# A hybrid SSD and attention layer: two products of each SSD chunk placed behind the copy of B on VectorE

## The chip, the cores and the metric

The kernel runs on one core of a Trainium2 chip. The metric is device time in microseconds (us), given as the median of several executions. The engines are called by the profile's names: PE (TensorE), DVE (VectorE), ACT (ScalarE), POOL (GpSimd) and SP (SyncE, which only issues DMAs here). PEld is PE's weight load.

## The reference, cut to what matters

One layer for 1024 tokens of width 1024: a Mamba-2 mixer (SSD) and multi-head latent attention side by side, merged by gates, then a gated MLP. The change lies in the SSD. For each of 4 groups (8 heads of 64 channels, a state of 128) the sequence is taken in 8 chunks of 128 tokens:

```python
seg = a_cum[..., :, None] - a_cum[..., None, :]
decay_in = jnp.exp(jnp.where(causal, seg, -jnp.inf))
scores = jnp.einsum('bclgn,bcsgn->bcgls', cc, bc)
y_diag = jnp.einsum('bcgls,bcgels,bcsgep->bclgep', scores, decay_in, xc)
chunk_states = jnp.einsum('bclgn,bcgel,bclgep->bcgepn', bc, decay_to_end, xc)
y_off = jnp.einsum('bclgn,cbgepn,bcgel->bclgep', cc, prev, jnp.exp(a_cum))
```

## The kernel before, in words

All products are in float32, most of them as three passes with operands split into a high and a low part (`mm3`, lines 175 to 177). So PE has long runs of 128x512 matmuls, named `lin` after their PSUM tile. The weights of a `lin` tile come by DMA into `wraw` (issued by SP, line 160), ACT casts them to the high part `whi` (line 153), and POOL subtracts to get the low part `wlo` (line 154).

In the SSD stage the loop runs over 4 groups and in each over 8 chunks; I write (g, c) for group g and chunk c. `ssd_steps` calls three functions in turn. `ssd_inputs` for the next chunk lets PE transpose x into `xp` and B into `sp` and form the scores; then DVE makes `xdt` (line 855), the masked scores `sm` (847), `xde` (860), the copy `bt` of B (863) and the product `seg` of decays and scores (864). ACT takes the exponential of `abc` (866), and DVE multiplies it by C (867). `ssd_state` is the PE product `sn` of `bt` and `xde` (874) that adds to the state (DVE, 881). `ssd_output` is the run of PE products `yp` (891 and 896) from `seg` and `abc`, then line 903 on DVE. Between these calls PE is given `lin` matmuls of other work: the convolution inputs of the next group (`conv_tile`, with lines 808 to 817 on ACT and DVE), z tiles (330) and, in the last group, tiles of the attention output (`mla_tiles`, with casts on line 146, subtractions on line 148 and line 1034).

`ssd_finish` runs a Newton iteration for the norm of the group before or of this group's first half: nine small DVE steps on 128x4 elements (lines 123 to 125, three times), called small steps below.

The order on an engine is not the order of the program text. A scheduler places each instruction by its own estimate of when inputs are ready, and every engine then works strictly in that order. `behind(name)` adds a dependence without a semaphore: the instruction just written must come later in its engine's order than the one named. PE's order is fixed in this way over the whole program (lines 1563 to 1570).

Of the kernel before, what the change touches and what calls it, by code (L numbers as in the profile page):

```python
# [72 lines left out]
def tile_hybrid_layer(ctx: ExitStack, tc: tile.TileContext, x, cols, cons, w_main, w_small, w_uq, w_ukv,  # L73
# [53 lines left out]
    def behind(name):  # L127

        ins = nc.cur_bb.bb.instructions[-1]
        if name:  # L130
            tc.add_manual_dep(ins, name, mybir.DependencyInfo(
                mybir.DependencyClass.NoSync, mybir.DependencyReason.DATA), reason="order")
        return ins.name

    def last(engine):
        return [ins for ins in nc.cur_bb.bb.instructions if ins.engine == engine][-1].name
# [635 lines left out]
    with tc.tile_pool(name="dp", bufs=2) as dp, tc.tile_pool(name="psx", bufs=1, space=PSUM) as psx, \  # L772
# [10 lines left out]
        def abc_load(n):  # L783

            if n < GROUPS * NT:
                g, c = divmod(n, NT)
                t = dp.tile([P, 8, P], F32, name="abc", bufs=3)
                nc.gpsimd.dma_start(out=t, in_=ac_d[c, 8 * g:8 * g + 8, :].partition_broadcast(P))
                abcs.append(t)
# [42 lines left out]
        def ssd_inputs(g, c):  # L832
            Bt, Ct, xs = chan[16 + g], chan[20 + g], chan[g]
            cs = slice(c * P, (c + 1) * P)
            hs = slice(8 * g, 8 * g + 8)
            abc_load(g * NT + c + 1)
            abc = abcs.pop(0)
            xp = psx.tile([P, 512], F32, name="xp")
            for j in range(4):
                PE.transpose(xp[:, j * P:(j + 1) * P], xs[:, j, cs], ident)  # L840
            sp = psx.tile([P, 512], F32, name="sp")
            PE.matmul(sp[:, 0:P], lhsT=Bt[:, cs], rhs=Ct[:, cs], start=True, stop=True)
            if c < NT - 1:
                PE.transpose(sp[:, 256:384], Bt[:, cs], ident)

            sm = dp.tile([P, P], F32, name="sm_")
            V.scalar_tensor_tensor(sm, sp[:, 0:P], 0.25, tri, op0=ALU.mult, op1=ALU.mult)
            seg = dp.tile([P, 8, P], F32, name="seg")
            for hd in range(8):
                S.activation(seg[:, hd, :], abc[:, hd, :], AF.Relu, bias=acum[:, c, 8 * g + hd:8 * g + hd + 1],  # L850
                             scale=-1.0)
            S.activation(seg, seg, AF.Exp, scale=-1.0)
            xv = xp.rearrange("p (h d) -> p h d", d=64)
            xdt = dp.tile([P, 512], F32, name="xdt")
            V.tensor_tensor(xdt.rearrange("p (h d) -> p h d", d=64), xv,
                            dtt[:, c, hs].unsqueeze(2).broadcast_to([P, 8, 64]), op=ALU.mult)
            xde = bt = None
            if c < NT - 1:
                xde = dp.tile([P, 512], F32, name="xde")
                V.tensor_tensor(xde.rearrange("p (h d) -> p h d", d=64), xv,  # L860
                                dte[:, c, hs].unsqueeze(2).broadcast_to([P, 8, 64]), op=ALU.mult)
                bt = dp.tile([P, P], F32, name="bt")
                V.tensor_copy(bt, sp[:, 256:384])
            V.tensor_tensor(seg, seg, sm.unsqueeze(1).broadcast_to([P, 8, P]), op=ALU.mult)
            if c > 0:
                S.activation(abc, abc, AF.Exp)
                V.tensor_tensor(abc, abc, Ct[:, cs].unsqueeze(1).broadcast_to([P, 8, P]), op=ALU.mult)
            return abc, seg, xdt, xde, bt

        def ssd_state(g, c, inp, st):  # L870
# [48 lines left out]
        def ssd_steps(g):  # L919
            st = None  # L920
            nxt = ssd_inputs(g, 0)
            yield
            for c in range(NT):
                inp = nxt
                nst = None
                if c < NT - 1:
                    nst = ssd_state(g, c, inp, st)
                    if c:
                        ssd_squares(g, c - 1)
                    yield  # L930
                    nxt = ssd_inputs(g, c + 1)
                    yield
                else:
                    ssd_squares(g, c - 1)
                ssd_output(g, c, inp, st)
                st = nst
                yield
# [129 lines left out]
        for n, _ in enumerate(conv_group(0)):  # L1067
# [3 lines left out]
            if n == 33:  # L1071
                name = last(mybir.EngineType.DVE)
# [581 lines left out]
```

## Time and profile before

| | |
|---|---|
| Median of 3 runs | 2227.03 us (2224.92 to 2229.38) |
| The profiled execution, its own time | 2224.44 us |
| Its span | 2222.6 us |
| PE busy | 2173.7 us, 98% of the span |
| DVE busy | 1430.4 us, 64% |
| ACT, POOL busy | 1012.4 us (46%), 822.4 us (37%) |
| Mean granted clock of PE | 0.996 of full speed |

The profiled execution took 1.8 us more than its span. Times in the rows count from the start of the span; the SSD stage lies between 800 and 1260 us.

### The profile page before, as it was taken

To read this page: it belongs to the slowest core of one execution; us is meant where nothing else is said; L and a number is where in the kernel's file an instruction comes from. 1 tells how busy PE (TensorE), PEld (TensorE's weight loads), DVE (VectorE), ACT (ScalarE), POOL (GpSimd) and SP (SyncE) were. 2 spreads that over 40 slices of the span, in tenths; PEclk is the share of its full clock that TensorE was granted. 3 is DMA by queue.
4 is the path that set the end of the run, shared out by engine and by line. 5 is a ranking of instruction groups with operands and counts; after the bars stand their busy time and mean duration, and the time that the engine had idled before them with its cause. 6 is when DMAs were issued, how large, how long until landed. Compare 5 with 4: busy or idle time off the path is not lost.

```text
span 2222.6 us, 31323 instructions
## 1 busy us (share of the span) xinstructions
PE 2173.7 (98%) x11488; PEld 1765.2 (79%) x11488; DVE 1430.4 (64%) x2496; ACT 1012.4 (46%) x1852; POOL 822.4 (37%) x911
## 2 busy tenths in 40 slices
PE   8999999999999999999999999999899999999999
PEld 6777777777777887878878889889688888888887
DVE  4466656666672469898876746546977777764432
ACT  5345454445444346666554424335544444443320
POOL 2244423443343237665455311012555555510000
PEclk9999999999999999999999999999999999999999
DMA  4121111111213224544276566543222222247531
GB/s 146 54 68 49 40 48 63 50 45 39 69 43 130 68 76 152 181 162 167 95 227 207 178 223 203 166 162 95 67 95 86 81 81 86 76 142 246 201 130 67
DMA packets 112714, 253.57 MB, mean 114 GB/s; under 512 B 13168, under 2 KB 19248, under 8 KB 112560
## 3 DMA queue, kind: packets, MB, share of 16 engines
q1 hardware_dynamic: 99008, 210.54, 28.6%
q0 software_dynamic: 11008, 37.76, 5.3%
q10 hardware_dynamic: 2544, 3.28, 0.4%
q8 instruction: 90, 1.47, 0.3%
q14 instruction: 64, 0.52, 0.1%
HBM read 194.63 MB, written 56.89 MB: 113 GB/s over the span
## 4 chain that ended last, share of the span: by engine, by line
PE 75%; DVE 13%; ACT 4%; DMA 3%; issue 2%; POOL 1%; SPq 0%; DVEq 0%; ACTq 0%; POOLq 0%
PE lin L175 12%; PE lin L177 12%; PE lin L176 12%; PE dps L177 8%; PE dps L175 8%; PE dps L176 8%; PE pv L670 2%; PE s L175 2%; PE s L176 1%; PE s L177 1%; PE s L627 1%; PE yp L891 1%; PE sn L874 1%; DMA wraw<-in_w_ssd 1%; DVE qk L588 1%
## 5 line engine op out<-in xcount | busy, mean ns | idle before, releaser
L175 PE MATMUL lin<-h,whi 128*128 128x512 f32 x1440 | 592.4, 411 | 0.0
L177 PE MATMUL lin<-h,wlo 128*128 128x512 f32 x1440 | 564.0, 392 | 0.0
L176 PE MATMUL lin<-h,whi 128*128 128x512 f32 x1440 | 563.0, 391 | 0.0
L175 PEld LDWEIGHTS lin<-h,whi 128*128 128x128 f32 x1440 | 271.4, 188 | 81.6 <-issue 33.4
L177 PEld LDWEIGHTS lin<-h,wlo 128*128 128x128 f32 x1440 | 270.7, 188 | 59.8 <-DVE wlo L154 0.2
L176 PEld LDWEIGHTS lin<-h,whi 128*128 128x128 f32 x1440 | 271.9, 189 | 53.2 <-issue 7.0
L153 ACT CAST whi<-wraw 128x512 fp32r<-128x512 f32 x276 | 166.6, 619 | 281.4 <-PE lin L176 131.6
L154 POOL TENSOR_TENSOR wlo<-wraw,whi 128x512 fp32r<-128x512 f32 x134 | 192.1, 1450 | 185.1 <-ACT whi L153 177.6
L659 ACT ACTIVATE e<-s 128x512 f32<-128x512 f32 (+1 forms) x192 | 93.7, 493 | 164.6 <-DVE s L657 137.7
L664 POOL TENSOR_TENSOR acc<-acc,e 128x512 f32<-128x512 f32 (+3 forms) x80 | 79.6, 995 | 230.8 <-ACT e L659 217.7
L154 DVE TENSOR_TENSOR wlo<-wraw,whi 128x512 fp32r<-128x512 f32 x142 | 99.2, 714 | 94.4 <-ACT whi L153 94.3
L154 DVE TENSOR_TENSOR h<-ar,h 128x1024 fp32r<-128x1024 f32 x40 | 48.7, 1225 | 108.8 <-ACT h L153 108.7
L850 ACT ACTIVATE seg<-abc,acum 128x128 f32<-128x128 f32 x256 | 80.6, 392 | 48.3 <-PE yp L891 42.3
L153 ACT CAST h<-ar 128x1024 fp32r<-128x1024 f32 x40 | 42.1, 1056 | 124.8 <-PE lin L176 115.7
L176 PE MATMUL dps<-wlo,h 128*128 128x512 f32 x240 | 93.4, 389 | 0.0
L175 PE MATMUL dps<-whi,h 128*128 128x512 f32 x240 | 93.4, 389 | 0.0
L177 PE MATMUL dps<-whi,h 128*128 128x512 f32 x240 | 93.4, 389 | 0.0
L812 DVE SCALAR_TENSOR_TENSOR xg<-craw,cl,xg 128x1024 f32<-128x1024 f32 x48 | 73.8, 1537 | 27.4 <-ACT xg L810 26.9
L664 DVE TENSOR_TENSOR acc<-acc,e 128x512 f32<-128x512 f32 (+3 forms) x80 | 53.5, 668 | 41.0 <-ACT e L659 40.4
L1140 ACT CAST xhi<-ur 128x512 fp32r<-128x512 f32 (+1 forms) x41 | 34.1, 832 | 89.5 <-PE dps L176 79.5
L670 PE MATMUL pv<-e,vt 128*64 128x512 f32 (+3 forms) x384 | 72.9, 499 | 0.0
L175 PE MATMUL s<-qh,kh 97*128 97x512 f32 (+1 forms) x192 | 68.5, 357 | 2.0 <-ACT qh L644 1.1
(587 smaller groups left out, 5189.5 us busy)
## 6 DMA issues: line engine op xcount, KB each, us to landing
wraw<-in_w_main SPq DMA_DIRECT2D x112, 256.0 KB, 3.1
ur<-in_w_up SPq DMA_DIRECT2D x44, 512.0 KB, 3.5
ar<-a_d SPq DMA_DIRECT2D x40, 512.0 KB, 5.1
abc<-ac_d POOLq DMA_DIRECT2D x32, 512.0 KB, 5.2
wraw<-in_w_ssd SPq DMA_DIRECT2D x64, 256.0 KB, 2.8
wraw<-in_w_down SPq DMA_DIRECT2D x44, 256.0 KB, 3.8
a_d<-uc SPq DMA_DIRECT2D x22, 512.0 KB, 2.6
g_d<-lt SPq DMA_DIRECT2D x32, 256.0 KB, 2.8
```

Source lines behind the costliest of these rows:

```text
L153: S.copy(hi, raw)
L154: (eng or V).tensor_sub(lo, raw, hi.bitcast(F32))
L175: PE.matmul(ps, lhsT=ah, rhs=bh, start=first, stop=False, **more)
L176: PE.matmul(ps, lhsT=ah, rhs=bl, start=False, stop=False, **more)
L177: PE.matmul(ps, lhsT=al, rhs=bh, start=False, stop=last, **more)
L588: V.tensor_tensor(qk[:, :, 2 + hd, 0:64], qk[:, :, 2 + hd, 0:64], rr[:, :, 2 + hd:3 + hd].broadcast_to([P, 4, 64]), op=ALU.mult)
L659: S.activation(e[:, c0:512], ps[:, 0:w], AF.Exp)
L664: (V if hd else G).tensor_tensor(accs[hd][:, c0:512], accs[hd][:, c0:512], e[:, c0:512], op=ALU.add)
L670: PE.matmul(pv[hd * 64:(hd + 1) * 64, c0:512], lhsT=vt[:, j, hd * 64:(hd + 1) * 64], rhs=es[hd][:, c0:512], start=first, stop=last)
L812: V.scalar_tensor_tensor(c, raw[:, k:k + T], col(cw + k), c, op0=ALU.mult, op1=ALU.add)
L850: S.activation(seg[:, hd, :], abc[:, hd, :], AF.Relu, bias=acum[:, c, 8 * g + hd:8 * g + hd + 1], scale=-1.0)
L1140: S.copy(hi, r)
```

## The change

The instruction written last before the product of line 864 is the copy `bt` (in chunk 7, which has none, the product `xdt`). Both are on DVE. The two DVE products, `seg` and `abc`, must now come behind it in DVE's order. No arithmetic changes, and PE's order is the same.

```diff
                 bt = dp.tile([P, P], F32, name="bt")
                 V.tensor_copy(bt, sp[:, 256:384])
+
+            name = behind(None)
             V.tensor_tensor(seg, seg, sm.unsqueeze(1).broadcast_to([P, 8, P]), op=ALU.mult)
+            behind(name)
             if c > 0:
                 S.activation(abc, abc, AF.Exp)
                 V.tensor_tensor(abc, abc, Ct[:, cs].unsqueeze(1).broadcast_to([P, 8, P]), op=ALU.mult)
+                behind(name)
             return abc, seg, xdt, xde, bt
```

Below the change the line numbers rise: 864 becomes 866, 866 becomes 869, 867 becomes 870, and later ones rise by 4.

DVE at (0,6), before. The small steps of the first half's norm stand among the steps of the chunk:

```order
L867 TENSOR_TENSOR abc<-abc,chan 128x1024
L124 TENSOR_TENSOR rsa<-rsa,grr 128x4
L125 SCALAR_TENSOR_TENSOR grr<-rsa,grr 128x4
L855 TENSOR_TENSOR xdt<-xp,dtt 128x512
L123 SCALAR_TENSOR_TENSOR rsa<-grr,rsv 128x4
L847 SCALAR_TENSOR_TENSOR sm__8880<-sp,cn 128x128
L124 TENSOR_TENSOR rsa<-rsa,grr 128x4
L860 TENSOR_TENSOR xde<-xp,dte 128x512
L125 SCALAR_TENSOR_TENSOR grr<-rsa,grr 128x4
L863 COPY bt<-sp 128x128
```

And DVE at the same place with the change:

```order
L125 SCALAR_TENSOR_TENSOR grr<-rsa,grr 128x4
L123 SCALAR_TENSOR_TENSOR rsa<-grr,rsv 128x4
L124 TENSOR_TENSOR rsa<-rsa,grr 128x4
L125 SCALAR_TENSOR_TENSOR grr<-rsa,grr 128x4
L855 TENSOR_TENSOR xdt<-xp,dtt 128x512
L847 SCALAR_TENSOR_TENSOR sm__8880<-sp,cn 128x128
L860 TENSOR_TENSOR xde<-xp,dte 128x512
L863 COPY bt<-sp 128x128
L866 TENSOR_TENSOR seg<-seg,sm__8880 128x1024
L870 TENSOR_TENSOR abc<-abc,chan 128x1024
```

The `abc` product moved from ahead of `xdt` to behind `seg`, and all nine small steps now stand ahead of `xdt`, where three stood before. At (1,6) six stand ahead of it now, and three did before.

DVE at (3,0), the first chunk of the last group, before:

```order
L330 SCALAR_TENSOR_TENSOR lt<-lt,lin 128x512
L867 TENSOR_TENSOR abc<-abc,chan 128x1024
L148 TENSOR_TENSOR h<-lt,h 128x512
L1034 SCALAR_TENSOR_TENSOR rb<-rb,lin 128x512
L855 TENSOR_TENSOR xdt<-xp,dtt 128x512
L847 SCALAR_TENSOR_TENSOR sm__11491<-sp,cn 128x128
L860 TENSOR_TENSOR xde<-xp,dte 128x512
L863 COPY bt<-sp 128x128
```

And with the change:

```order
L330 SCALAR_TENSOR_TENSOR lt<-lt,lin 128x512
L148 TENSOR_TENSOR h<-lt,h 128x512
L1038 SCALAR_TENSOR_TENSOR rb<-rb,lin 128x512
L855 TENSOR_TENSOR xdt<-xp,dtt 128x512
L847 SCALAR_TENSOR_TENSOR sm__11491<-sp,cn 128x128
L860 TENSOR_TENSOR xde<-xp,dte 128x512
L863 COPY bt<-sp 128x128
```

The `abc` product that stood here belongs to the next chunk, (3,1), and now follows that chunk's `seg`.

ACT somewhat ahead of (3,0), before, from the last exponential of `seg` in group 2:

```order
L852 ACTIVATE seg<-seg 128x1024
L914 ACTIVATE sq__11378<-xg 128x512
L329 ACTIVATE lt<-lin 128x512
L146 CAST h<-rb 128x512 x3
L153 CAST whi<-wraw 128x512 x2
L850 ACTIVATE seg<-abc,acum 128x128 x5
```

And with the change:

```order
L852 ACTIVATE seg<-seg 128x1024
L153 CAST whi<-wraw 128x512
L329 ACTIVATE lt<-lin 128x512
L146 CAST h<-rb 128x512
L918 ACTIVATE sq__11378<-xg 128x512
L146 CAST h<-rb 128x512 x2
L153 CAST whi<-wraw 128x512
L850 ACTIVATE seg<-abc,acum 128x128 x8
```

The first of the two weight casts moved from behind three casts of `h` to directly behind the exponential. On POOL the first of the two subtractions (line 154) and on SP the first of the two weight loads that follow (line 160) moved ahead in the same way.

## Rows read from the trace of the kernel before

**Rows 1.** The page: busy time, share of the span, instructions.

```profile
PE 2173.7 (98%) x11488; PEld 1765.2 (79%) x11488; DVE 1430.4 (64%) x2496; ACT 1012.4 (46%) x1852; POOL 822.4 (37%) x911
```

**Rows 2.** Waits, 800 to 1260 us: waiter, releaser, us in total, times, longest.

```profile
PE sn L874 <- DVE bt L863: 5.1, 3, 3.1
...
PEld sn L874 <- DVE bt L863: 6.8, 4, 3.5
```

**Rows 3.** Timeline of PE: start, duration, line, operation, [idle before, releaser].

```profile
884.95 1.13 PE L874 MATMUL sn<-xde,bt 128*128 128x512 f32 x2
...
954.72 1.12 PE L874 MATMUL sn<-xde,bt 128*128 128x512 f32 x2 [0.47 <-DVE bt L863]
...
996.18 1.13 PE L874 MATMUL sn<-xde,bt 128*128 128x512 f32 x2 [1.58 <-DVE bt L863]
...
998.54 0.39 PE L175 MATMUL lin<-h,whi 128*128 128x512 f32 x1
...
1152.95 1.75 PE L874 MATMUL sn<-xde,bt 128*128 128x512 f32 x2 [3.07 <-DVE bt L863]
...
1156.92 0.39 PE L175 MATMUL lin<-h,whi 128*128 128x512 f32 x1
```

**Rows 4.** Windows: length, busy of PE, PEld, DVE, ACT, POOL, granted clock.

```profile
996.00:1000.00 4.00, 3.82 (x15) 2.83 (x16) 3.97 (x8) 0.04 (x1) 0.00 (x0) 1.00 0.67 197
1153.00:1157.00 4.00, 4.00 (x9) 2.56 (x10) 4.00 (x4) 1.62 (x3) 3.39 (x4) 0.57 0.68 196
```

**Rows 5.** Groups of DVE, 795 to 1260 us: busy, mean ns, idle before.

```profile
L867 DVE TENSOR_TENSOR abc<-abc,chan 128x1024 f32<-128x1024 f32 x27 | 35.0, 1297 | 12.6 <-ACT abc L866 12.6
...
L860 DVE TENSOR_TENSOR xde<-xp,dte 128x512 f32<-128x512 f32 x28 | 19.0, 680 | 0.0
```

**Rows 6.** Timeline of DVE at (3,0).

```profile
1148.64 1.47 DVE L867 TENSOR_TENSOR abc<-abc,chan 128x1024 f32<-128x1024 f32 x1 [3.18 <-ACT abc L866]
1150.03 0.68 DVE L148 TENSOR_TENSOR h<-lt,h 128x512 fp32r<-128x512 f32 x1
...
1151.23 0.68 DVE L855 TENSOR_TENSOR xdt<-xp,dtt 128x512 f32<-128x512 f32 x1
...
1152.62 0.28 DVE L863 COPY bt<-sp 128x128 f32<-128x128 f32 x1
```

**Rows 7.** Timeline of ACT ahead of (3,0).

```profile
1137.57 0.62 ACT L153 CAST whi<-wraw 128x512 fp32r<-128x512 f32 x1
...
1147.02 0.62 ACT L153 CAST whi<-wraw 128x512 fp32r<-128x512 f32 x1 [2.29 <-DMA wraw<-in_w_mla]
...
1148.51 0.60 ACT L146 CAST h<-lt 128x512 fp32r<-128x512 f32 x1
```

**Rows 8.** Timeline of POOL and of SP's queue ahead of (3,0).

```profile
1140.09 1.30 POOL L154 TENSOR_TENSOR wlo<-wraw,whi 128x512 fp32r<-128x512 f32 x1
...
1141.42 0.33 SPq L160 DMA_DIRECT2D wraw<-in_w_mla  x1
```

**Rows 9.** Timeline of DVE at (1,6).

```profile
990.35 1.21 DVE L867 TENSOR_TENSOR abc<-abc,chan 128x1024 f32<-128x1024 f32 x1
991.48 1.25 DVE L124 TENSOR_TENSOR rsa<-rsa,grr 128x4 f32<-128x4 f32 x1
...
993.90 0.68 DVE L855 TENSOR_TENSOR xdt<-xp,dtt 128x512 f32<-128x512 f32 x1
...
995.11 0.15 DVE L124 TENSOR_TENSOR rsa<-rsa,grr 128x4 f32<-128x4 f32 x1
...
995.84 0.28 DVE L863 COPY bt<-sp 128x128 f32<-128x128 f32 x1
```

**Rows 10.** Timeline of POOL at (1,6): the first of two `wlo`, then both merged.

```profile
990.37 2.34 POOL L154 TENSOR_TENSOR wlo<-wraw,whi 128x512 fp32r<-128x512 f32 x1
...
990.37 3.59 POOL L154 TENSOR_TENSOR wlo<-wraw,whi 128x512 fp32r<-128x512 f32 x2
```

**Rows 11.** Timeline of DVE at (0,6) and at (1,3).

```profile
884.62 0.28 DVE L863 COPY bt<-sp 128x128 f32<-128x128 f32 x1
...
947.95 2.28 DVE L812 SCALAR_TENSOR_TENSOR chan<-craw,cl,chan 128x1024 f32<-128x1024 f32 x1 [0.77 <-ACT chan L810]
```

## The prediction

> **What bounds the kernel now.** I read the page's busy times first: PE is busy for 2173.7 us of a span of 2222.6 us [rows 1]. Its `lin` matmuls follow each other without a break, so a change on DVE can only win or lose time where PE stops, or where its clock drops. PE's order is the same in both kernels. So the next view is what PE waited for in the SSD stage. There is one entry: the state product `sn` waited for the copy `bt`, 5.1 us in 3 places; counted at its weight loads it is 6.8 us in 4 places [rows 2]. Between these two figures lies all that PE loses to DVE in this stage. The timeline of PE gives the places: 0.47 us at (1,3), 1.58 us at (1,6), 3.07 us at (3,0), and at (0,6) a start 0.05 us after `bt` ended at 884.90 us, with almost no idle time of PE [rows 3, 11]. The other 24 `sn` had their `bt` in time.
>
> The longest stop costs more than itself. After it the granted clock is 0.57 over 4 us, about the lower of PE's levels (1.2 GHz, and 2.4 GHz at 1.00); after the stop of 1.58 us it stayed at 1.00 [rows 4]. From the start of `sn` to the third `lin` product of line 175 behind it took 1156.92 - 1152.95 = 3.97 us there, and 998.54 - 996.18 = 2.36 us at (1,6) [rows 3]. The slow clock cost about 1.6 us.
>
> **What the change does.** The tie of `seg` does nothing by itself: it stood behind `bt` already. What moves is the `abc` product, from ahead of the chunk's `xdt` to behind its `seg`. It takes 1.30 us on average in 27 of its 28 places, and DVE also stood still ahead of it for 12.6 us in total, until ACT's exponential was done [rows 5]. That idle time held up everything behind it on DVE, `bt` above all. At the new place the product comes some 3 us later (`xdt`, `sm`, `xde`, `bt` and `seg` run first), and the longest wait was 3.18 us [rows 6], so I cost the wait at the new place at nothing. If ACT were late all the same, what would queue behind the product is line 903 (which frees the PSUM of `yp`) and the convolution steps of line 812, for which ACT's line 816 and then its copies of `lin` wait. The consumer of `abc` itself, the second products of `yp`, come after the next `sn`, many microseconds later, except in chunk 7, where `abc` will end about when `seg` did before.
>
> Four places, one after the other.
>
> (3,0). Before, DVE waits 3.18 us for ACT and then spends 1.47 us on a product of the next chunk, ahead of the steps that PE is waiting for [rows 6]. Without it the next step, line 148, has to wait for the cast on ACT that starts at 1148.51 us and takes 0.60 us [rows 7]: it can start at about 1149.1 instead of 1150.03. That is 0.9 us, the lower bound. But the ACT cast itself is late because of a weight cast ahead of it that waited 2.29 us for a load [rows 7]. This load was issued at 1141.42 us, right after POOL's second `wlo` had ended at 1141.39 [rows 8]; that followed the first `wlo`, and both followed two casts on ACT that began at 1137.57 [rows 7]. In the new order the first cast, the first `wlo` and the first load all stand further ahead, so the second `wlo` no longer queues behind the first: it can start about when its cast has ended, some 1.8 us earlier (1140.09 against 1137.57 + 0.62 + a little). If the load lands as much earlier, 0.9 + 1.8 = 2.7 us of the 3.07 are gone. I take 2.2 us: the load goes out into the same traffic. A stop of 0.9 us is shorter than the 1.58 us that left the clock at 1.00, so the 1.6 us of slow clock go as well. Together 3.8 us. Bounds: 0.9 us (slow clock kept) and 3.07 + 1.6 = 4.7 us.
>
> (1,6). Before, the small steps took 1.25 us where POOL worked and 0.15 us where it didn't [rows 9]: a step of DVE on SBUF and one of POOL take turns. The same is seen from the other side: `abc` ran for its 1.21 us from 990.35, and POOL's first `wlo`, started at 990.37, took 2.34 us, while the two together took 3.59 us, so the second took some 1.25 us [rows 9, 10]. `xdt`, which reads PSUM, ran at its usual 0.68 us during POOL's work. The change takes 1.21 us of `abc` away, but three more small steps now come ahead of `xdt`. Each costs up to 1.25 us while POOL still has work queued. I take a loss of 0.2 us. Bounds: the whole stop of 1.58 us gone, if the small steps come before POOL's run; or 1.5 us longer (three steps behind POOL, 3.75 us, less the 1.21 us and about 1 us in which POOL is finished earlier).
>
> The Trainium skill, "SBUF — State Buffer", section "Who interferes with whom", says that a DVE instruction with two SBUF inputs contends with a GpSimd instruction that reads SBUF, and that the loser blocks for the whole instruction. By that rule the small steps wait for every queued POOL step and the sum is the one below; without it, six small steps at 0.15 us would let `bt` end before PE asks for it at 994.6 us (996.18 - 1.58), and the sum would be better by about 1.8 us. The trace agrees with the rule: 1.25 us against 0.15 us.
>
> (0,6). Here nine small steps stand ahead of `xdt` now, so `xdt` to `bt`, which ran while POOL worked, come after its run: 1.67 us by the same steps at (3,0) (1151.23 to 1152.90), plus some 0.35 us of small steps, less the 1.21 us of `abc`. A loss of 0.8 us; bounds: next to nothing to win, since PE had hardly stopped, and 2 us lost, if DVE comes later into this run.
>
> (1,3). `abc` ends at 947.18 (945.97 and 1.21 us), but the step behind it then waits 0.77 us for ACT's line 810 anyway [rows 11]. Removing `abc` there lengthens that wait. I take 0, bounds 0.5 us either way.
>
> **The sum.** -3.8 + 0.2 + 0.8 + 0 = -2.8 us. Against the profiled execution's own time, 2224.44 us, that is 2221.6 us; this execution lies 2.6 us below the median of the runs, 2227.03 us, to which the forecast must compare: 2224.2 us. That is -0.13%, less than the 0.2% (4.5 us) that a measurement of this kernel can tell from no change.
>
> **Rivals.**
>
> All the stops go: DVE saves the 12.6 us of waiting, and this head start carries to (0,6), (1,3) and (1,6), so that the small steps come ahead of POOL's run. Then 5.1 to 6.8 us and the 1.6 us of slow clock are won, 7.5 us in the middle: 2219.5 us. For it speaks that the product ahead of (1,6), in chunk 5, is one of those that waited. Against it: at (1,3) the steps wait for ACT and not for DVE, and the product now stands ahead of the convolution steps that come before the small ones.
>
> Slower: at (0,6) and (1,6) the small steps come into POOL's run later than before, because the `abc` product of chunk 5 now stands between its `seg` and the convolution steps and meets POOL's `wlo` there. Each place then loses about 2 us. At (1,6) the stop would be 3.6 us, longer than the one at which the clock fell, and 1.6 us more would go; at (3,0) only the 0.9 us would be won: 2 + 2 + 1.6 - 0.9 = 4.7 us, 2231.7 us. It decides from a stop at (1,6) of about 3 us.
>
> Next to nothing happens: 24 of 28 `sn` have no wait, and if the load at (3,0) lands no earlier and the clock still falls there, the 0.9 us are eaten by (0,6): 2227 us.
>
> **Chances and range.** The forecast, with what lies around it down to 4.4 us won, 42%; next to nothing 12%; all or nearly all the stops gone, 32%; slower 14%. So faster by over 0.2%: 0.32; within 0.2%: 0.54; slower: 0.14. The range takes the middle of the fast rival, 2219.5 us, and reaches up to 2230.5 us, short of the slow rival's full price: about 1 in 10 is left out on each side.
>
> **What would show it.** In the profile after: `abc` directly behind `seg`, its 12.6 us of waiting for ACT nearly gone; the wait of `sn` at (3,0) under 1.5 us and the granted clock at 1.00 behind it; at (0,6) a stop of about 1 us that is new, at (1,6) one of 1.5 to 2 us, with small steps of 1.2 us ahead of `xdt`. The prediction is wrong if PE waits for something new in the SSD stage (a `lin` tile for ACT's copy, `yp` for `abc`), if the stop at (3,0) stays over 2 us, or if (0,6) and (1,6) show no stop.

## The result, and the profile after

The changed kernel takes 2231.03 us (median of 19 runs, 2223.67 to 2236.13); the kernel before, on the same chips, 2225.87 us (19 runs, 2219.03 to 2229.38). The ratio is 1.0023, with a 95% interval of 1.0014 to 1.0031. So the change is slower by about 5 us, just over what can be told from no change. The forecast was 2224.2 us, with a chance of 14% for slower. Two executions of `e1` below went at a granted clock of 0.66 and took over 3200 us; they are left out of its median.

The profiled execution of the changed kernel is no help at first sight. It is the fastest of the 19 runs, at 2223.67 us, and its span is 2221.8 us, 0.8 us less than that of before. I therefore set a second profiled execution of the same program beside it (the run `e12_after_again`, span 2228.6 us), which lies nearer the median.

This is the line of busy times on the page of the first execution; it answers to [rows 1] and is almost the same:

```profile
PE 2173.8 (98%) x11488; PEld 1764.9 (79%) x11488; DVE 1438.7 (65%) x2496; ACT 1010.7 (45%) x1852; POOL 821.5 (37%) x911
```

PE's waits from 800 to 1260 us in the first execution, as in [rows 2]:

```profile
PE sn L878 <- DVE bt L863: 5.4, 3, 1.9
PE yp L895 <- DVE seg L866: 1.0, 1, 1.0
PE yp L900 <- DVE abc L870: 1.0, 2, 0.7
```

And in the second:

```profile
PE sn L878 <- DVE bt L863: 7.6, 3, 4.0
PE yp L895 <- DVE seg L866: 1.0, 1, 1.0
PE yp L900 <- DVE abc L870: 1.0, 2, 0.7
```

Two things are to be seen. `yp` waits for `seg` and `abc`, which it never did before. And the longest wait of `sn` is 1.9 us in one execution and 4.0 us in the other. The timeline of PE shows the places, here for the first execution, as in [rows 3] (start, duration, line, operation, idle time before and its releaser):

```profile
885.62 1.12 PE L878 MATMUL sn<-xde,bt 128*128 128x512 f32 x2 [1.65 <-DVE bt L863]
...
901.01 0.44 PE L895 MATMUL yp<-seg,xdt 128*64 128x128 f32 x4 [0.99 <-DVE seg L866]
902.14 0.44 PE L900 MATMUL yp<-abc,st 128*64 128x128 f32 x4 [0.69 <-DVE abc L870]
...
998.28 1.13 PE L878 MATMUL sn<-xde,bt 128*128 128x512 f32 x2 [1.95 <-DVE bt L863]
...
1013.30 0.44 PE L900 MATMUL yp<-abc,st 128*64 128x128 f32 x4 [0.27 <-DVE abc L870]
...
1154.25 1.13 PE L878 MATMUL sn<-xde,bt 128*128 128x512 f32 x2 [1.82 <-DVE bt L863]
...
1156.61 0.39 PE L175 MATMUL lin<-h,whi 128*128 128x512 f32 x1
```

The stops are at (0,6), in chunk 7 of group 0 (two), at (1,6), in chunk 7 of group 1, and at (3,0). The one at (1,3) is gone. In the second execution all of them are the same to 0.02 us but the last:

```profile
1156.58 2.08 PE L878 MATMUL sn<-xde,bt 128*128 128x512 f32 x2 [4.00 <-DVE bt L863]
...
1161.01 0.63 PE L175 MATMUL lin<-h,whi 128*128 128x512 f32 x1
```

From `sn` to the third product of line 175 behind it took 1156.61 - 1154.25 = 2.36 us in the first execution and 1161.01 - 1156.58 = 4.43 us in the second. The windows behind the stop at (3,0) say why (columns as in [rows 4]; the granted clock is the third number from the end). First execution:

```profile
1154.00:1158.00 4.00, 3.75 (x15) 2.76 (x16) 4.00 (x4) 2.67 (x5) 2.83 (x2) 1.00 0.72 234
```

Second execution:

```profile
1156.00:1160.00 4.00, 3.42 (x6) 2.10 (x7) 3.50 (x5) 2.51 (x5) 2.98 (x2) 0.50 0.74 219
```

The clock stayed at 1.00 (2.4 GHz) in the first and stood at 0.50 (1.2 GHz) in the second, which cost 2.1 us there.

What the forecast expected on DVE did come. `abc` follows `seg`, and its 12.6 us of waiting for ACT [rows 5] are gone; but DVE now waits 17.6 us for PE's `xp` ahead of `xdt`, against 10.4 us before. DVE from 795 to 1260 us, before and then in the first execution of the change:

```profile
L855 DVE TENSOR_TENSOR xdt<-xp,dtt 128x512 f32<-128x512 f32 x32 | 21.9, 684 | 10.7 <-PE xp L840 10.4
...
L870 DVE TENSOR_TENSOR abc<-abc,chan 128x1024 f32<-128x1024 f32 x28 | 38.3, 1369 | 0.0
L855 DVE TENSOR_TENSOR xdt<-xp,dtt 128x512 f32<-128x512 f32 x32 | 21.9, 683 | 17.6 <-PE xp L840 17.6
```

Single executions differ by several us ahead of this stage: the first `sn` starts between 801.0 and 805.3 us in four executions of the order of before. So I compare below the stretch from the first `sn` to the last, at (3,6). It took 434.0 us before (805.28 to 1239.30), 434.7 us in the first execution of the change (804.31 to 1238.98) and 439.3 us in the second (804.40 to 1243.70).

### The profile page after: what moved, and what is told of

The parts are those of the page before. It is cut to its first block, busy times and chain, and to the rows that moved or that the text cites. A ratio compares the mean times of both kernels' runs of the same rounds, so it can differ in the third digit from the quotient of the medians.

```text
span 2221.8 us, 31334 instructions
## 1 busy us (share of the span) xinstructions
PE 2173.8 (98%) x11488; PEld 1764.9 (79%) x11488; DVE 1438.7 (65%) x2496; ACT 1010.7 (45%) x1852; POOL 821.5 (37%) x911
## 4 chain that ended last, share of the span: by engine, by line
PE 75%; DVE 14%; DMA 4%; ACT 4%; issue 2%; POOL 1%; SPq 0%; ACTq 0%; DVEq 0%; POOLq 0%
PE lin L175 13%; PE lin L177 12%; PE lin L176 12%; PE dps L175 7%; PE dps L177 7%; PE dps L176 7%; PE pv L670 2%; PE s L175 2%; PE s L176 1%; PE s L177 1%; PE s L627 1%; PE yp L895 1%; DMA wraw<-in_w_ssd 1%; PE sn L878 1%; DVE xg L812 1%
```

## The experiments

Seven runs repeat the order of the change or of before, the others tie `abc` in some chunks only, or move the small steps. Ratios are to the kernel before on the same chip, with the 95% interval.

**Which of the two ties.**

```diff
             V.tensor_tensor(seg, seg, sm.unsqueeze(1).broadcast_to([P, 8, P]), op=ALU.mult)
-            behind(name)
             if c > 0:
```

> Only the abc product is tied behind bt; the tie of seg is taken away. Every engine's order of instructions is that of the change. All theories: 2231 us median, ratio 1.0015 to 1.003. What its profile adds is a second execution of this order. Theory 'stops and clock' (the loss is the new stops of PE in chunks 6 and 7 of groups 0 and 1, and in a typical execution the granted clock falls behind one or more of them, at some 1.6 us each, which the profiled execution of the change happened to escape): sn at (0,6) and (1,6) wait 1.6 to 2.2 us again, and in an execution of about 2231 us the granted clock is well under 1.00 in the few us behind one of the stops. Rival 'elsewhere' (the stops are worth only some 0.8 us together, and the rest is lost by moved loads, casts or at other stages): the granted clock stays 1.00 behind all the stops of the SSD stage in such an execution, and lies lower outside 795 to 1260 us.

2229.5 us, ratio 1.0010 (1.0001 to 1.0020), under the 1.0015 that was expected. Every stop ahead of (3,0) is that of the change to 0.02 us. At (3,0) it was 4.43 us and the clock was at 0.50 in the 4 us behind; the stretch took 439.3 us. So the clock fell indeed, but at (3,0) and not behind one of the new stops: both theories were off in the place.

```diff
                 V.tensor_tensor(abc, abc, Ct[:, cs].unsqueeze(1).broadcast_to([P, 8, P]), op=ALU.mult)
-                behind(name)
             return abc, seg, xdt, xde, bt
```

> Only the seg product is tied behind bt; abc is free, as before. Every engine's order is that of the kernel before. All theories: 2226 us, ratio 0.999 to 1.001. It shows what the measurement tells from no change, and its profile is a second execution of the order of before: sn waits of about 0.1 us at (0,6), 0.5 at (1,3), 1.6 at (1,6) and 3.1 at (3,0), with the granted clock lower behind the last.

2225.95 us, ratio 0.9995 (0.9986 to 1.0004), with stops of 0.46, 1.55 and 3.08 us at (1,3), (1,6) and (3,0). The tie of `seg` does nothing, as forecast.

**Which chunks.**

```diff
-                behind(name)
+                if c >= 6:
+                    behind(name)
```

> abc is tied behind bt (in chunk 7 behind xdt) only in chunks 6 and 7 of each group; in chunks 1 to 5 it is free, as before. Theory 'stops and clock': the stop at (3,0) of 3.1 us with its 1.6 us of slow clock stays, and the new stops come on top: 1.6 us at (0,6), 0.4 at (1,6), 0.9 + 0.9 and 0.5 us at yp of (0,7) and (1,7), with slow clock behind one or two of them: 2226 + 4 + 1.6 to 3.2 = 2231 to 2233 us, ratio 1.0025 to 1.0035. Rival 'elsewhere': the stops alone, without the gain at (3,0), which is 4 us, but nothing more: the loss comes from the other chunks, and this kernel is at 2226 to 2229 us.

2228.83 us, ratio 1.0009 (1.0000 to 1.0018): the upper end of the rival's range, though the stop at (3,0) was 4.63 us with slow clock. The profile says more. `sn` at (0,6):

```profile
881.81 1.13 PE L879 MATMUL sn<-xde,bt 128*128 128x512 f32 x2 [0.85 <-DVE bt L863]
```

The waits of `yp` in chunk 7 are 1.00, 0.69 and 0.24 us, as with the whole change, but (0,6) has only half of its stop.

```diff
-                behind(name)
+                if c < 6:
+                    behind(name)
```

> abc is tied behind bt only in chunks 1 to 5; in chunks 6 and 7 it is free. Theory 'stops and clock': the stops at (0,6), (1,6) and chunk 7 are as before, and the gain at (3,0) is kept (1.2 us of the stop, 1.6 us of slow clock): 2226 - 2.8 = 2223 us, ratio 0.998 to 0.9995. Rival 'elsewhere': the loss is in what the ties of chunks 1 to 5 move (loads, casts, small steps), and this kernel is at 2228 to 2231 us, ratio over 1.001.

2223.59 us, ratio 0.9987 (0.9979 to 0.9996). The place of the loss is right: without the ties of chunks 6 and 7 it becomes a small gain. But (0,6) is not as before:

```profile
882.26 1.13 PE L879 MATMUL sn<-xde,bt 128*128 128x512 f32 x2 [0.80 <-DVE bt L863]
```

0.85 and 0.80 us from the two parts make the 1.65 us of the whole change. One half comes from the order at the place itself, the other from DVE arriving late there. At (1,6) the two parts do not add up in this way: 1.91 us with the ties of chunks 6 and 7 alone, 1.01 us with those of chunks 1 to 5 alone, and 1.95 us with all.

```diff
-                behind(name)
+                if c < 5:
+                    behind(name)
```

> abc is tied behind bt only in chunks 1 to 4. With the ties of chunks 1 to 5 the stop at (0,6) was 0.96 us, at (1,6) 1.17 and at yp of (1,7) 0.95, and 2223.6 us were measured. If it is the product of chunk 5 that pushes the convolution steps and these the steps of chunk 6, (0,6) goes back to 0.2 us, (1,6) to 1.7 and (1,7) to under 0.3, while (1,3) stays without a stop: 2222 to 2224 us, ratio 0.998 to 0.9993. If not, the stops are as with chunks 1 to 5 and the time is at 2223.6 us or above.

2226.07 us, ratio 0.9995 (0.9986 to 1.0004). A miss: (0,6) kept its 0.80 us, and (1,6) rose to 2.68 us. So the ties of chunks 1 to 4 make DVE late at (0,6) without that of chunk 5.

**Which groups.**

```diff
-                behind(name)
+                if g < 2:
+                    behind(name)
```

> The change in groups 0 and 1 alone; in groups 2 and 3 abc is free, and each engine's order there is that of before. Theory 'chunks 6 and 7' (the loss is the stops there: 1.8 + 1.15 + 0.9 + 2.1 + 0.5 us with the change against 0.2 + 0.3 + 0.6 + 1.7 us before, 3.6 us more): 2226 + 3.6 = 2229.6 us, ratio 1.001 to 1.002, and the stop at (3,0) stays near 3.2 us. Rival 'the late load' (the loss is at (3,0), where with the change the weight load of line 160 goes out 4 us later than before and the stop was 4.6 us with slow clock in a second execution; stops ahead of it in groups 0 and 1 only give the loads time): 2226 to 2227.5 us, ratio under 1.0007.

```diff
-                behind(name)
+                if g >= 2:
+                    behind(name)
```

> The change in groups 2 and 3 alone; in groups 0 and 1 abc is free, and each engine's order there is that of before. Theory 'chunks 6 and 7': no stop is added, the one at (3,0) is shorter than 3.2 us or about as long: 2223 to 2226.5 us, ratio 0.9985 to 1.0002. Rival 'the late load': the load goes out about 4 us later than before, the stop at (3,0) is 4 us or more, with slow clock: 2227.5 to 2230 us, ratio over 1.0007.

Groups 0 and 1 alone: 2228.76 us, ratio 1.0011 (1.0002 to 1.0019). Groups 2 and 3 alone: 2225.37 us, 0.9994 (0.9985 to 1.0003). In the same set the whole change was at 1.0018. What loss can be told from noise is in groups 0 and 1; the rival "the late load" as the sole cause fails, as the ratio of groups 2 and 3 is not over 1.0007. At (3,0) `e9`, whose groups 2 and 3 have the order of before, had a stop of 2.39 us behind one of 0.44 us (`lin`, line 330), with the clock at 1.00, where near 3.2 us was expected; `e10`, with the order of the change there, had 2.50 us, and the clock fell to 0.64 from 1151 to 1155 us. The two parts sum to +1.6 us and the whole to +4.2 us, but each has an uncertainty of 2 us.

**The place (3,0) alone.**

```diff
-                behind(name)
+                if (g, c) == (3, 1):
+                    behind(name)
```

> Only the abc product of (3,1) is tied behind its bt; nothing of groups 0 to 2 moves. Theory 'the product ahead of line 148' (what the forecast counted on at (3,0): without the product DVE waits there only for ACT's cast): the stop of sn at (3,0) is 0.9 us shorter than 3.2 us, about 2.3 us; if the granted clock stays at 1.00 behind it, 1.6 us more: 2223.5 to 2225 us, ratio 0.999 to 0.9996. Rival 'the load alone' (the stop at (3,0) is set by when the weight load of line 160 lands, and the product only fills the wait): the stop stays at 2.8 us or more, slow clock with it, and the time at 2226 us, ratio over 0.9996.

2225.11 us, ratio 0.9990 (0.9981 to 1.0000). The stop of `sn` was 1.68 us, but a `lin` product just ahead of it waited 0.83 us for line 330, which had no wait before; together 2.5 us. The clock stayed at 1.00. That is nearer to the first theory (2.3 us) than to its rival (2.8 us or more).

**The small steps.** They are written after the inputs of chunk 6 and tied behind its `bt`:

```diff
-            rsqrt_mean(rr, np_[:, 0:4], 512)
+            more = rsqrt_mean(rr, np_[:, 0:4], 512, not half)
             yield
+            if not half:
+                newton(*more, copied[0])
             yield
```

Here `newton` holds the nine steps, the first of each three tied behind `copied[0]`, the last `bt`.

> The kernel before, with abc free, but the nine small steps of each group's first half are written after the inputs of chunk 6 and tied behind its bt. Theory 'small steps in POOL's run' (bt is late at (1,6) because small steps ahead of it lose their turns to POOL): the stop at (1,6) of 1.6 us goes to under 0.3 us, so 2226 - 1.7 = 2224 us, ratio 0.999 to 0.9996. Rival 'the steps are late wherever they are': the nine steps behind bt now hold up seg or what follows it (line 903, the second product of np), and the stop comes back at yp of chunk 6 or 7 or at np: 2226 us or more.

> The change, and the nine small steps of each group's first half behind the bt of chunk 6. Theory 'small steps in POOL's run': the stops at (0,6) and (1,6), 1.8 and 2.1 us with the change, go to under 0.3 us each, so 2231 - 3.6 = 2227 us, ratio 0.9995 to 1.001; the waits of yp in chunk 7 (2.5 us) and the late load at (3,0) stay. Rival 'abc of chunk 5 pushes the convolution steps, and these push bt': the stops at (0,6) and (1,6) stay over 1 us, and the time at 2230 to 2231 us.

> Both of the last two edits of the kernel before: only abc of (3,1) tied, and the nine small steps of each group's first half behind the bt of chunk 6. If the two gains add up: 0.9 us (2.5 with the clock) at (3,0) and 1.7 us at (1,6): 2226 - 2.6 to 4.2 = 2222 to 2223.5 us, ratio 0.998 to 0.999. If one of the two rivals above holds: 2224 us or more.

2229.11 us, ratio 1.0013 (1.0002 to 1.0023), for the kernel before with this edit; 2228.33 us, 1.0013 (1.0003 to 1.0023), for the changed kernel with it; 2226.80 us, 0.9999 (0.9990 to 1.0009), with the single tie at (3,1). In all three no `sn` waits at (0,6) or (1,6): the small steps had held `bt` up there. But all three times miss the gain that was hoped for, because the waiting goes to the next consumer. `yp` in chunk 7 of groups 0 and 1, kernel before with the edit:

```profile
898.89 0.44 PE L899 MATMUL yp<-seg,xdt 128*64 128x128 f32 x4 [0.87 <-DVE seg L872]
...
1009.68 0.44 PE L899 MATMUL yp<-seg,xdt 128*64 128x128 f32 x4 [1.52 <-DVE seg L872]
```

In the first of the three the stop at (3,0) was 4.10 us as well. In these three runs, where the steps stand decided only which product of PE waits for DVE. The rival "late wherever they are" is right.

**The same order again.** With `e1` and `e2` and the runs below, which have no edit, there are four profiled executions of the order of before and five of the order of the change.

> The changed kernel once more, for a third execution of its order and a ratio beside the other three. All theories: 2230 us, ratio 1.001 to 1.003; the stops in chunks 6 and 7 as in the two executions so far. The stop at (3,0), 1.98 us in one and 4.59 us in the other, follows the landing of the weight load that was issued at about 1145.3 us, after 4.0 and 6.3 us: it is again 2 us when the load takes about 4 us, and 4.6 us with slow clock when it takes about 6.

> The changed kernel, one more execution. If the late load is the usual case: the weight load lands over 5.5 us after its issue, the stop of sn at (3,0) is 4 us or more, with slow clock behind it, and 2229 to 2232 us. If the execution first profiled is as usual as the others: a stop of about 2 us and 2224 to 2227 us. In both cases sn starts 5.06 us after the weight cast that waited for the load, and the stops in chunks 6 and 7 are as before.

> As the run before it: a stop at (3,0) of 4 us or more and 2229 to 2232 us if the late load is usual, about 2 us and 2224 to 2227 us if not.

> The kernel before, one more execution. If its stop at (3,0) is steady: 3.0 to 3.5 us as in the two executions so far, sn starting 5.93 us after the weight cast, and 2224 to 2228 us. If it has the same spread as the changed order: under 2.5 or over 4 us.

> As the run before it: 3.0 to 3.5 us at (3,0) if steady, under 2.5 or over 4 us if it has the spread of the changed order.

The first of them gave 2230.47 us, ratio 1.0018 (1.0010 to 1.0027); the single times of the others are 2236.21, 2225.79, 2228.32 and 2223.94 us. The two executions of before are as steady as was expected; `e13` is slower than either of its branches, and `e14`, with a stop of 3.06 us and the clock at 1.00, fits neither. For each execution I worked out at (3,0): the issue of the weight load whose cast is the last ahead of `sn`, how far it lies ahead of the time at which PE asks for `bt` (start of `sn` less its wait), the time to the start of the cast (which waits for the load), and from the cast to `sn`. The second of two merged loads is taken to start at the end of their row less its own 0.33 us.

| execution | load ahead of PE's asking | load to cast | cast to `sn` | wait | clock behind | stretch |
|---|---|---|---|---|---|---|
| before | 8.46 | 5.60 | 5.93 | 3.07 | 0.57 | 434.0 |
| e2 | 7.86 | 5.01 | 5.93 | 3.08 | 0.50 | 435.2 |
| e15 | 7.87 | 5.12 | 5.94 | 3.19 | 0.50 | 435.1 |
| e16 | 7.61 | 4.69 | 5.92 | 3.00 | 0.50 | 435.1 |
| after | 7.22 | 3.98 | 5.06 | 1.82 | 1.00 | 434.7 |
| e1 | 6.95 | 6.32 | 5.06 | 4.43 | 0.50 | 439.3 |
| e12 | 7.32 | 6.26 | 5.06 | 4.00 | 0.50 | 439.3 |
| e13 | 6.96 | 5.77 | 5.06 | 3.87 | 0.50 | 440.4 |
| e14 | 6.96 | 4.58 | 5.44 | 3.06 | 1.00 | 436.7 |

The wait is load to cast plus cast to `sn` less the first column, in each row. So the short stop of the first profile is a load that happened to land in 4.0 us, and 4 us of stop are at least as usual. The order of before is steadier here, 3.0 to 3.2 us in four executions; but `e9`, which has it at (3,0) and stopped longer ahead of it, had 2.39 us.

**A version that is faster.** Ties in chunks 1 to 5, in all groups once more, and in groups 2 and 3 alone:

```diff
-                behind(name)
+                if g >= 2 and c < 6:
+                    behind(name)
```

> abc is tied behind bt only in chunks 1 to 5 of groups 2 and 3; each engine's order in groups 0 and 1 is that of before. If the gain of the ties in chunks 1 to 5 lies at (3,0): the stops in groups 0 and 1 are those of before (0.2, 0.3, 0.6, 1.7 us), at (3,0) there are two of together about 2.5 us with the clock at 1.00 behind them, and the time is 2222 to 2224.5 us, ratio 0.998 to 0.9994. If it was chance: 2225 to 2227 us, and over 3 us of stop at (3,0).

> The kernel with the ties in chunks 1 to 5 of all groups once more. If its gain is real: 2222.5 to 2224.5 us again, ratio 0.998 to 0.9995, and at (3,0) again two stops of together about 2.5 us. If it was chance: 2225 us or more.

With groups 2 and 3 alone 2225.12 us, ratio 0.9993 (0.9983 to 1.0002); the stop at (3,0) was 2.85 us with the slow clock behind it, so that expectation fails. With all groups 2224.80 us, ratio 0.9990 (0.9981 to 0.9999), after 0.9987 before. Both its intervals lie below 1, the second only just: the ties in chunks 1 to 5 make a kernel about 0.1% faster than before, and so some 0.2 to 0.3% faster than the change. Where that gain lies its second profile did not confirm: it has two stops at (3,0), of 2.29 us (`lin`, line 330) and 1.65 us, with the clock at 1.00, against 0.58 and 1.54 us in the first.

## Why the prediction was wrong

**What bounds the kernel, and the tie of `seg`.** Right: `sn` and now `yp` waiting for DVE are all that moved in PE's waits from 800 to 1260 us, and `seg` alone does nothing (0.9995).

**(3,0), -3.8 us.** This term failed, in its step on the load: "the second `wlo` no longer queues behind the first: it can start about when its cast has ended, some 1.8 us earlier". The lower bound was right to 0.03 us: without `abc` the way from the cast to `sn` is 5.06 us in place of 5.93, 0.87 us less, in four of the five executions (5.44 us in the other). The second `wlo` did start about when its cast had ended. But that cast came later, and so the load did not go out earlier. ACT's order puts three casts of `h` between the two weight casts, and these waited for their own loads. ACT of the first execution:

```profile
1135.70 0.62 ACT L153 CAST whi<-wraw 128x512 fp32r<-128x512 f32 x1
...
1138.53 0.62 ACT L146 CAST h<-rb 128x512 fp32r<-128x512 f32 x1 [1.72 <-DMA rb<-at_d]
...
1141.61 0.62 ACT L146 CAST h<-rb 128x512 fp32r<-128x512 f32 x1 [1.92 <-DMA rb<-at_d]
1142.62 0.62 ACT L146 CAST h<-rb 128x512 fp32r<-128x512 f32 x1 [0.39 <-DMA rb<-at_d]
1143.15 0.62 ACT L153 CAST whi<-wraw 128x512 fp32r<-128x512 f32 x1
```

POOL and SP's queue follow:

```profile
1143.87 1.31 POOL L154 TENSOR_TENSOR wlo<-wraw,whi 128x512 fp32r<-128x512 f32 x1
```

```profile
1145.21 0.33 SPq L160 DMA_DIRECT2D wraw<-in_w_mla  x1
```

The load went out at 1145.21 us, against 1141.42 before [rows 8]. PE was later there too; against PE's asking, the load lost 0.9 us of its start in the mean (7.1 us ahead, from 7.95), as much as the shorter way from the cast gains. By its numbers (1137.57 + 0.62) the step had the second cast begin where the two had begun before, right behind the three casts of `h`; it took these to run when they had run before. The change itself delays them. In chunk 7 of group 2 the moved `abc` product now stands ahead of DVE's line 148, which frees `rb` for their loads. Before:

```profile
1129.00 1.29 DVE L148 TENSOR_TENSOR h<-rb,h 128x512 fp32r<-128x512 f32 x2
1129.71 0.92 SPq L139 DMA_DIRECT2D rb<-at_d  x2
```

And in the first execution of the change:

```profile
1130.88 1.22 DVE L870 TENSOR_TENSOR abc<-abc,chan 128x1024 f32<-128x1024 f32 x1
...
1133.22 1.28 DVE L148 TENSOR_TENSOR h<-rb,h 128x512 fp32r<-128x512 f32 x2
1134.28 1.17 SPq L139 DMA_DIRECT2D rb<-at_d  x2
```

Counted from PE's asking for `bt`, the last of these loads went out 19.6 us ahead in four executions of before and 17.2 to 17.7 us ahead in five of the change. The ties of chunks 6 and 7 alone (`e3`) give 17.5 us, and the weight load then goes out 7.0 us ahead; those of chunks 1 to 5 alone (`e4`) leave 20.4 and 9.3 us. And in the four profiles where (3,1) is tied but chunk 7 of group 2 is not (`e4`, `e5`, `e17`, `e18`) the stop of `sn` was 1.54, 1.68, 2.85 and 1.65 us, with up to 2.29 us of `lin` ahead of it, and the clock fell in `e17` alone.

The mean wait at (3,0) is 3.09 us in four executions before and 3.44 us in five with the change. The slow clock came in four of four and in three of five. So the gain of 3.8 us came out as about nothing, with waits of the change that spread from 1.82 to 4.43 us.

**(0,6), +0.8 us.** The step was right and the sum too small, since the stop is 1.65 us. DVE of the first execution:

```profile
880.12 1.21 DVE L124 TENSOR_TENSOR rsa<-rsa,grr 128x4 f32<-128x4 f32 x1
881.36 1.22 DVE L125 SCALAR_TENSOR_TENSOR grr<-rsa,grr 128x4 f32<-128x4 f32 x1
...
883.62 0.16 DVE L124 TENSOR_TENSOR rsa<-rsa,grr 128x4 f32<-128x4 f32 x1
...
885.29 0.28 DVE L863 COPY bt<-sp 128x128 f32<-128x128 f32 x1
```

and POOL:

```profile
880.02 2.54 POOL L154 TENSOR_TENSOR wlo<-wraw,whi 128x512 fp32r<-128x512 f32 x2
```

The small steps take 1.2 us each beside POOL's `wlo` and 0.16 us when POOL's run, with line 883 behind the `wlo`, is over; `xdt` to `bt` come after them. The trace agrees here with the rule of the Trainium skill, "SBUF — State Buffer", section "Who interferes with whom", that the forecast cited. That order alone costs 0.85 us (the ties of chunks 6 and 7 alone): my 0.8. The other 0.80 us (the ties of chunks 1 to 5 alone) is DVE coming later into POOL's run, which I had as the bound of 2 us and not as the value. The traces let it be followed back to the product of chunk 4. Before:

```profile
848.40 1.23 DVE L867 TENSOR_TENSOR abc<-abc,chan 128x1024 f32<-128x1024 f32 x1 [1.11 <-ACT abc L866]
```

First execution of the change:

```profile
851.37 2.29 DVE L870 TENSOR_TENSOR abc<-abc,chan 128x1024 f32<-128x1024 f32 x1
```

```profile
850.32 2.27 POOL L985 TENSOR_TENSOR rb<-rb,nb 128x512 f32<-128x512 f32 x1
852.54 4.50 POOL L154 TENSOR_TENSOR wlo<-wraw,whi 128x512 fp32r<-128x512 f32 x2
```

At its new place it takes 2.29 us beside POOL, and the convolution steps behind it (line 812) start 2.3 us later, counted from the first `sn`. At line 812 of chunk 5 0.8 us of this are left, with that chunk's product tied (`e4`) or free (`e11`).

**(1,6), +0.2 us,** came out as 1.94 against 1.56 us in the mean of the executions of each order: +0.4. **(1,3), 0,** came out as -0.5 us, its bound: the stop is gone in all five.

**Chunk 7, 0 us.** This is the second step that failed: "except in chunk 7, where `abc` will end about when `seg` did before". DVE in chunk 7 of group 0, first execution:

```profile
896.22 2.71 DVE L962 SCALAR_TENSOR_TENSOR xg<-xg,cl,np__8996 128x512 f32<-128x512 f32 x4
898.86 0.28 DVE L847 SCALAR_TENSOR_TENSOR sm__9025<-sp,cn 128x128 f32<-128x128 f32 x1
899.06 0.67 DVE L855 TENSOR_TENSOR xdt<-xp,dtt 128x512 f32<-128x512 f32 x1
899.65 1.21 DVE L866 TENSOR_TENSOR seg<-seg,sm__9025 128x1024 f32<-128x1024 f32 x1
900.79 1.21 DVE L870 TENSOR_TENSOR abc<-abc,chan 128x1024 f32<-128x1024 f32 x1
```

`seg` had no slack ahead of `yp` before, and now it is late by 0.99 us. DVE gained nothing from the product that is missing ahead of line 962, because it now waits for ACT's line 816 where the product had stood:

```profile
894.78 1.52 DVE L817 SCALAR_TENSOR_TENSOR xg<-craw,xg 128x1024 f32<-128x1024 f32 x1 [1.13 <-ACT craw L816]
```

`abc`, which had been made ahead of line 962, starts when `seg` ends, so the second products wait 0.69 us more. With 0.24 to 0.27 us in chunk 7 of group 1 (none in `e13`) that is 1.9 us in the mean. It comes with the ties of chunks 6 and 7 alone, and not with those of chunks 1 to 5, which leave 0.8 us at (1,7) only.

**The sum.** In place of -3.8 + 0.2 + 0.8 + 0 = -2.8 us the waits give +0.35 (3,0), +1.65, +0.4, -0.5 and +1.9, which is +3.8 us, less some tenths for a clock that falls somewhat more rarely. The stretch grew by 3.2 us in the mean (434.9 to 438.1) and 4.2 us in the median (435.1 to 439.3). The three timed comparisons of this order give 5.2, 2.9 and 4.2 us between medians.

**The rival "slower"** had the right sign, 2231.7 us, and the right place: the small steps come into POOL's run later than before. Its price at (1,6) was wrong (2 us and a slow clock; it was 0.4 us, with a slow clock in one of five executions and in `e9`, which has the same order there), and of chunk 7 it knew nothing. So it is luck that its sum lies 0.7 us from the measured median. The product of chunk 5, which it blames, was free in `e11`, and 0.80 us of stop at (0,6) were there all the same; that of chunk 4 meets POOL in just the way that it describes. "All the stops go" failed: of the 12.6 us that DVE no longer waited for ACT, 7.2 came back as longer waits for `xp` (17.6 against 10.4 us), and no head start reached (0,6). "Next to nothing" had (3,0) right in most executions, a load that lands no earlier and a clock that still falls, but it gave the loss at (0,6) no more than 0.9 us and chunk 7 nothing.

**What was said would show it.** A stop of 1.82 us and the clock at 1.00 at (3,0), in the first profile, were near the signs that the forecast had named. They were chance. The other sign, that PE waits for something new (`yp`), said rightly that the forecast was wrong.

What stays open is how much of the gain of the ties of chunks 1 to 5 is the clock at (3,0): it stayed at 1.00 in both their profiles and fell in all four of before, but the second profile shows no shorter stop. The way from the `abc` product of chunk 4 to the 0.80 us at (0,6) is read from traces; no run ties or frees that product alone. That the second weight cast, moved ahead of the casts of `h`, would bring the load forward was not tried.

## What to carry to other kernels

When a product is moved behind others on a full engine, price each consumer that now comes sooner than the product, down to the last chunk of a group, where no other work lies between. Follow also what the moved product now stands ahead of: here a step that frees a buffer, and with it a load 20 us ahead of the stop. An edit that spares an engine a wait gains only what the next wait on that engine leaves. And when the term that decides is a load that lands in time or doesn't, compare several profiled executions over a stretch between two fixed instructions before believing any: one execution here had the sign wrong.

## What was unexpected of the hardware

The same load, issued at the same place among the same others, took 3.98 to 6.32 us until its cast could start. The 4 us behind its issue, first execution of the change:

```profile
1145.20:1149.20 4.00, 4.00 (x22) 3.32 (x21) 0.58 (x1) 3.40 (x9) 3.96 (x6) 1.00 0.85 283
```

and in the second:

```profile
1145.20:1149.20 4.00, 4.00 (x20) 3.28 (x20) 0.69 (x1) 3.20 (x7) 3.96 (x7) 1.00 0.87 217
```

The last two numbers are the busy share of the DMA engines and GB/s. They were as busy, 0.85 and 0.87, and moved 283 and 217 GB/s. What slows them is not settled.

Nor does the length of a stop decide whether the clock falls behind it. Behind a stop of 3.50 us it stayed at 1.00 (the kernel of `e8`, at (3,0)):

```profile
1152.00:1156.00 4.00, 3.91 (x15) 2.92 (x16) 4.00 (x4) 2.20 (x4) 3.38 (x2) 1.00 0.68 221
```

Behind one of 1.94 us (the kernel of `e13`, at (1,6)) it fell:

```profile
999.00:1003.00 4.00, 3.79 (x8) 2.56 (x9) 4.00 (x6) 0.65 (x1) 0.00 (x0) 0.60 0.68 256
```

The same stop of 1.94 to 1.95 us left it at 1.00 in the first execution, as 1.58 us did before [rows 4].
